# The conditioning of layer 0 in a two-layer hybrid backbone step: the shift as TensorE products, x loaded first, and half of the products issued between the input's products

## The chip, the core and the metric

The kernel runs on one core of a Trainium2 chip. The metric is the device time of one execution in microseconds (us), as the median of several runs. A core has five engines that each run their own instruction list in order and wait for one another through semaphores: TensorE (PE, matmuls; PEld are its weight loads), VectorE (DVE), ScalarE (ACT), GpSimd (POOL) and SyncE (SP), which here issues most of the DMA loads.

## What is computed

The reference is one step of a two-layer model on 512 latent and 128 context tokens, 640 in all, with 1024 channels. What the change touches is the start of layer 0: two vectors for each kind of token, a shift and a scale, are made from a conditioning vector, and the normalised input is modulated with them before the input projection.

```python
def branch_inputs(x, cond, w_ada, b_ada, norm_g, w_in):
    shift, scale, gate = jnp.split(jax.nn.silu(cond) @ w_ada + b_ada, 3, axis=-1)
    xm = rms_norm(x, norm_g) * (1.0 + scale) + shift
    parts = jnp.split(xm @ w_in, SPLIT_POINTS, axis=-1)
    return gate, parts
```

`cond` is `c` for the latent tokens and `c_ctx` for the context tokens, so each product with `w_ada` (1024 x 3072 for a layer) has two rows. All is fp32. After that come, in each layer, three token mixers (neighbourhood attention, latent attention, a Fourier mix), their gates and the output projections.

## The kernel before, in words

Activations stand with channels on the partitions: x is 8 tiles of 128 channels by 640 tokens, columns 0 to 511 latent and 512 to 639 context. An fp32 product is made of three matmuls of rounded parts: each operand is split in a high part (ScalarE copies it to `fp32r`) and a low part (VectorE or GpSimd subtracts the high part), and high x high, low x high and high x low are summed in PSUM. A weight unit of 1024 x 128 is loaded by `unit` (512 KB into `wr`), split by ScalarE into `wh` and by GpSimd into `wl`.

`start` does the conditioning of layer 0 and the first three weight units of the input projection (`ckv`, `ql0`, `ql1`; the last of them is split in halves into tiles named `k`). Its parts, with the line numbers of the kernel before:

- Loads (lines 285 to 290, and the string `ORD` from line 359 on): SyncE issues the eight x tiles with seven small loads between them, then follows `ORD`: A to D are four quarters of the scale part of `w_ada` (`wsc`, 8 tiles of 128 x 512 for each half of the channels), U the next weight unit, P the shift columns of channel tile 0 (`wsp`), S the transposed shift columns of one further channel tile (`wsh`).
- `cond` broadcast (lines 293 to 299): four matmuls with one row of ones (L295) put the conditioning vector on all partitions, and ScalarE's tanh (L297) and VectorE (L298) make silu of it (`sil`).
- `rms` (L177 to L192): ScalarE squares each x tile, VectorE adds them up, TensorE sums over the partitions with a matrix of ones, and the reciprocal root `y` is made from that (L164 to L167).
- `products` (L323): fp32 matmuls of `cc` (silu of the two conditioning rows, 128 x 2 for each k) with a weight tile, into two rows of PSUM; ScalarE copies the row (L325), TensorE transposes it in pieces of 128 (L327), and VectorE makes from them `am` = (1 + scale) x norm weight (L333), or `mod`, the shift of channel tile 0 (L331). There are 8 products of 512 columns for each half of the scale, and 8 of 128 columns for the shift of channel tile 0.
- `shift(n)` (L339): for the channel tiles 1 to 7 VectorE multiplies a transposed weight tile with `sil` and sums along the row, four times for a channel tile.
- `modulate` (L255, L259, L263, L265): VectorE forms h x am x y, ScalarE adds the shift, and the result is split in `xh` and `xl`; for a channel tile in `LOP` the low part is GpSimd's work (L144), else VectorE's. Then 18 matmuls of 320 columns (L390 to L392) add this channel tile to six accumulators in PSUM, two for each unit.

The code's order is only a wish: the build arranges each engine's list by its own schedule, so that matmuls of a channel tile can stand between products. `tc.issue_after(i)` keeps an instruction behind `i`. PSUM has eight banks: `s` takes two of them, `g` three, `pt` two and `o` one. The first matmul behind `start` is one of the units' gemms (L149, `g<-wh,xh` of 272 columns); from there on the two kernels have the same work.

Of the kernel before, what the change touches and what calls it, by code (L numbers as in the profile page):

```python
# [10 lines left out]
F32 = mybir.dt.float32  # L11
F32R = mybir.dt.float32r
AF = mybir.ActivationFunctionType
# [15 lines left out]
NS = 1  # L29
NF = (5, 4, 0, 0)  # L30
LOP = range(5)
# [7 lines left out]
ORD = "ASBSUPCUDSSSSUSS"  # L39
# [39 lines left out]
def step_kernel(ctx: ExitStack, tc: tile.TileContext, io):  # L79
# [197 lines left out]
    def start():  # L277
# [5 lines left out]
        rows = [sb_t("xl") for _ in range(4)]  # L283
        small = [(cc[:, 0], io["condT"])]
        small += [(rows[j][0:1, :512], io["cond"][j // 2:j // 2 + 1, (j % 2) * 512:(j % 2 + 1) * 512]) for j in range(4)]
        small += [(vecs, io["vecs"]), (bada, io["bada"])]
        for k in range(KD):
            sp.dma_start(out=h[k], in_=io["xt"][k])
            if k < len(small):
                sp.dma_start(out=small[k][0], in_=small[k][1])  # L290
        silu2(cc[:, 1], cc[:, 0])
        sil = []
        for j in range(4):
            g = psum("g" if j < 3 else "o")
            pe.matmul(g, ones[0:1], rows[j][0:1, :512], start=True, stop=True)  # L295
            t = sb_t("m", F32, 512)
            act.activation(out=t, in_=g, func=AF.Tanh, scale=0.5)  # L297
            dve.scalar_tensor_tensor(out=t, in0=t, scalar=1.0, in1=g, op0=ALU.add, op1=ALU.mult)  # L298
            sil.append(t)
        hg, gb = (sb.tile([128, KD], F32, name=n) for n in ("hg", "gb"))  # L300
        dve.tensor_scalar(hg, vecs[:, 0, 0:8], 0.5, None, ALU.mult)
        dve.scalar_tensor_tensor(out=gb, in0=bada[:, 0, 8:16], scalar=1.0, in1=vecs[:, 0, 0:8], op0=ALU.add, op1=ALU.mult)
        rms(h, 1.0 / D, y, ((0, T),), ("pt", "pt"))
        sc = psum("s")
        ws = []

        space = iter(["pt"] * 6 + ["q"] * 4 + ["lt"] * 5 + ["k"] + ["v"] * 8 + ["l"] * 2 + ["ob"] * 2 + ["gt"] + ["k"] * 4)
        wsc, wsh = [[], []], {}

        def load_scale(hf, ks):  # L310
            for k in ks:
                wsc[hf].append(sb_t(next(space))[:, :512])
                sp.dma_start(out=wsc[hf][k], in_=io["wsc"][hf, k])

        def load_shift(n):
            wsh[n] = [sb_t(next(space)) for _ in range(2)]
            for hf in range(2):
                sp.dma_start(out=wsh[n][hf][:, :512], in_=io["wsh"][n - NS, :, hf * 512:(hf + 1) * 512])

        def products(ws, n, col, n0):  # L320

            for k in range(KD):
                pe.matmul(sc[0:2, 0, :n * 128], cc[:, 1, k], ws[k], start=k == 0, stop=k == KD - 1)  # L323
            row = sb_t("fh")
            act.activation(out=row[0:2, :n * 128], in_=sc[0:2, 0, :n * 128], func=AF.Copy)  # L325
            for i in range(n):
                pe.transpose(sc[:, 1, col + 2 * i:col + 2 * i + 2], row[0:2, i * 128:(i + 1) * 128], ident[0:2, 0:2])  # L327
            for i in range(n):
                src, m = sc[:, 1, col + 2 * i:col + 2 * i + 2], n0 + i
                if col == 16:  # L330
                    dve.tensor_scalar(mod[:, 0, :, m], src, 0.5, bada[:, 0, m:m + 1], ALU.mult, ALU.add)  # L331
                else:
                    dve.tensor_scalar(am[:, 0, :, m], src, hg[:, m:m + 1], gb[:, m:m + 1], ALU.mult, ALU.add)  # L333

        def shift(n):
            for i in range(2):
                for hf in range(2):
                    col = mod[:, 0, i, n:n + 1]
                    dve.tensor_tensor_reduce(out=junk, in0=wsh[n][hf][:, :512], in1=sil[2 * i + hf], scale=0.5,  # L339
                                             scalar=bada[:, 0, n:n + 1] if hf == 0 else col,  # L340
                                             op0=ALU.mult, op1=ALU.add, accum_out=col)

        wsp = []
# [14 lines left out]

        later_shifts, names = iter(range(NS, KD)), iter(("ckv", "ql0", "ql1"))
        for o in ORD:  # L360
            if o in "ABCD":
                hf, q = divmod("ABCD".index(o), 2)
                load_scale(hf, range(4 * q, 4 * q + 4))
            elif o == "S":
                n = next(later_shifts, None)
                if n is not None:
                    load_shift(n)
            elif o == "U":
                ws.append(start_unit(next(names)))
            else:  # L370
                for k in range(KD if NS else 0):
                    wsp.append(sb_t("xh")[:, :NS * 128])
                    sp.dma_start(out=wsp[k], in_=io["wsp"][k])
        for n in later_shifts:
            load_shift(n)
        products(wsc[0], 4, 0, 0)
        if NS:
            products(wsp, NS, 16, 0)
        products(wsc[1], 4, 8, 4)
        xs = x_tiles()  # L380
        acc = [[psum("g"), psum("g")], [psum("g"), psum("o")], [psum("pt"), psum("pt")]]
        for n in range(KD):
            if n >= NS:
                shift(n)
            modulate(0, n, h[n], y, xs, ((0, T),), "pool" if n in LOP else "dve")
            for u in range(3):
                hi, lo = ws[u][0][n], ws[u][1][n]
                for i, (a, b) in enumerate(HALVES):
# [3 lines left out]
                    pe.matmul(o, hi, xs[1][n][:, a:b], start=False, stop=n == KD - 1)  # L392
# [712 lines left out]
```

## Time and profile before

| | before |
|---|---|
| median of 3 runs | 1474.37 us (1473.84 to 1475.03) |
| profiled execution | 1476.68 us |
| span of its trace | 1474.9 us, 1.8 us less |
| busy TensorE, VectorE, ScalarE, GpSimd | 96%, 65%, 48%, 35% |
| start (up to the first L149 matmul) | 0 to 69.3 us |

The span runs from the first to the last instruction of the profiled execution; the metric has some 1.8 us around it. A busy share is the time in which the engine had an instruction in work. TensorE's share is made of modelled ends of pipelined matmuls, so how long a row of matmuls takes is better read from the starts. Times in the trace are counted from the start of the span.

### The profile page before, as it was taken

What the parts mean: (1) busy time and instruction counts of PE and PEld (TensorE: products, weight loads), DVE (VectorE), ACT (ScalarE), POOL (GpSimd) and SP (SyncE); (2) the same over time, 40 slices, a digit from 0 to 9 for tenths busy, and PEclk for the clock granted to TensorE, in tenths of its full rate; (3) what the DMA queues carried; (4) which work ended last, traced back from release to release, by engine and by line L of the source; (5) the groups of instructions that cost most, each with busy time, mean ns of one, the idle gap of its engine ahead of it and who ended that gap; (6) DMA issues with size and microseconds to landing.
All of it is one profiled execution on the core that took longest, in us unless ns stands there. A gap on an engine that the chain in (4) does not pass through costs nothing.

```text
span 1474.9 us, 24841 instructions
## 1 busy us (share of the span) xinstructions
PE 1418.6 (96%) x9623; PEld 1368.5 (93%) x9623; DVE 955.0 (65%) x1903; ACT 705.7 (48%) x1440; POOL 512.0 (35%) x233
## 2 busy tenths in 40 slices
PE   7899999999999999989989999999999999999996
PEld 2799999999999899989989999999999999999996
DVE  7768567777648888784576554565643667753456
ACT  5353454554536565412355444554544565652243
POOL 3351222123232132247653423113222312224764
PEclk9999999999999999999999999999999999999998
DMA  9244224234334444764553322122232323355544
GB/s 322 108 145 134 96 95 137 73 114 137 127 123 132 143 144 133 235 220 160 191 183 92 110 78 100 59 79 91 75 132 101 95 98 123 122 171 208 163 160 144
DMA packets 84302, 197.33 MB, mean 134 GB/s; under 512 B 10068, under 2 KB 23764, under 8 KB 84184
## 3 DMA queue, kind: packets, MB, share of 16 engines
q1 hardware_dynamic: 76152, 178.71, 37.2%
q10 hardware_dynamic: 8032, 17.04, 3.0%
q8 instruction: 75, 1.23, 0.3%
q14 instruction: 43, 0.35, 0.1%
HBM read 165.67 MB, written 30.05 MB: 133 GB/s over the span
## 4 chain that ended last, share of the span: by engine, by line
PE 79%; DVE 10%; DMA 5%; issue 3%; ACT 1%; POOL 1%; SPq 0%; DVEq 0%; POOLq 0%; ACTq 0%
PE g L150 21%; PE g L151 21%; PE g L149 21%; PE pt L563 4%; DVE junk L242 2%; PE o L611 2%; PE o L612 2%; PE s L150 2%; PE s L151 2%; PE s L149 2%; DMA wr<-wt 1%; PE s L760 1%; PE s L761 1%; DMA ob<-br_d 1%; POOL wl L125 1%
## 5 line engine op out<-in xcount | busy, mean ns | idle before, releaser
L125 POOL TENSOR_TENSOR wl<-wr,wh 128x1024 fp32r<-128x1024 f32 (+2 forms) x173 | 427.2, 2474 | 896.9 <-ACT wh L124 842.8
L149 PE MATMUL g<-xh,wh 128*128 128x320 f32 (+2 forms) x1584 | 490.6, 310 | 4.3 <-DVE lt L416 2.7
L151 PE MATMUL g<-xh,wl 128*128 128x320 f32 (+2 forms) x1584 | 494.6, 312 | 0.0
L150 PE MATMUL g<-xl,wh 128*128 128x320 f32 (+2 forms) x1584 | 491.5, 311 | 0.0
L149 PEld LDWEIGHTS g<-xh,wh 128*128 128x128 f32 x1584 | 299.2, 189 | 7.4 <-issue 2.9
L151 PEld LDWEIGHTS g<-xh,wl 128*128 128x128 f32 x1584 | 299.3, 189 | 1.8 <-POOL wl L125 0.2
L150 PEld LDWEIGHTS g<-xl,wh 128*128 128x128 f32 x1584 | 298.2, 188 | 2.0
L124 ACT ACTIVATE wh<-wr 128x1024 fp32r<-128x1024 f32 (+2 forms) x173 | 182.3, 1055 | 177.3 <-PE g L150 91.0
L144 DVE TENSOR_TENSOR pt<-pt,pt 128x512 fp32r<-128x512 f32 (+2 forms) x176 | 101.2, 588 | 29.7 <-ACT pt L143 27.6
L678 DVE TENSOR_REDUCE st<-s 128x1 f32<-128x640 f32 x64 | 52.6, 822 | 96.4 <-PE s L151 96.1
L143 ACT ACTIVATE pt<-pt 128x512 fp32r<-128x512 f32 (+2 forms) x176 | 88.2, 517 | 52.2 <-PE pt L563 49.8
L549 DVE TENSOR_SCALAR p<-p,st 128x640 f32<-128x640 f32 (+3 forms) x160 | 101.3, 638 | 5.4 <-DVE st L548 0.5
L563 PE MATMUL pt<-ident,p 128*128 128x128 f32 x575 | 91.8, 273 | 1.2 <-DVE p L549 1.2
L150 PE MATMUL g<-wl,xh 128*128 128x272 f32 (+1 forms) x320 | 91.6, 286 | 0.7 <-POOL wl L125 0.7
L149 PE MATMUL g<-wh,xh 128*128 128x272 f32 (+1 forms) x320 | 91.3, 287 | 0.0
L151 PE MATMUL g<-wh,xl 128*128 128x272 f32 (+1 forms) x320 | 91.2, 286 | 0.0
L680 ACT ACTIVATE p<-s,st 128x640 f32<-128x640 f32 x64 | 50.9, 795 | 72.9 <-DVE st L678 72.6
L563 PEld LDWEIGHTS pt<-ident,p 128*128 128x128 f32 x575 | 71.9, 140 | 9.1 <-DVE p L549 1.4
L548 DVE RECIPROCAL st<-st 128x1 f32<-128x1 f32 x160 | 25.1, 160 | 61.5 <-ACT p L680 35.5
L242 DVE CUSTOM_DVE_ANT_0 junk<-a,sc,mod 128x512 bf16<-128x512 f32 x64 | 62.3, 974 | 3.8 <-DMA a<-wada 3.5
L149 PE MATMUL g<-k,wh 128*128 128x320 f32 (+2 forms) x176 | 57.0, 324 | 7.3 <-ACT xh L263 2.4
L782 ACT ACTIVATE p<-p,st 128x384 f32<-128x384 f32 (+1 forms) x64 | 42.8, 668 | 44.1 <-DVE st L780 43.9
(274 smaller groups left out, 2979.2 us busy)
## 6 DMA issues: line engine op xcount, KB each, us to landing
wr<-wt SPq DMA_DIRECT2D x158, 512.0 KB, 3.5
a<-wada SPq DMA_DIRECT2D x64, 256.0 KB, 2.8
gate_d<-lt ACTq DMA_DIRECT2D x48, 320.0 KB, 2.2
m<-bias SPq DMA_DIRECT2D x32, 320.0 KB, 3.2
br_d<-ob SPq DMA_DIRECT2D x24, 320.0 KB, 2.7
l<-br_d SPq DMA_DIRECT2D x16, 320.0 KB, 3.5
p<-gate_d SPq DMA_DIRECT2D x16, 320.0 KB, 6.9
lt<-gate_d SPq DMA_DIRECT2D x16, 320.0 KB, 4.4
```

What stands on the lines that cost most here:

```text
L124: act.activation(out=wh[:, :n], in_=r[:, :n], func=AF.Copy)
L125: pool.tensor_tensor(out=wl[:, :n], in0=r[:, :n], in1=wh[:, :n].bitcast(F32), op=ALU.subtract)
L143: act.activation(out=hi, in_=src, func=AF.Copy)
L144: (pool if e == "pool" else dve).tensor_tensor(out=lo, in0=src, in1=hi.bitcast(F32), op=ALU.subtract)
L149: pe.matmul(out, ah, bh, start=i == 0, stop=False)
L150: pe.matmul(out, ah, bl, start=False, stop=False)
L151: pe.matmul(out, al, bh, start=False, stop=i == n - 1)
L242: dve.tensor_tensor_reduce(out=junk, in0=w, in1=sc[:, i], scale=0.5, scalar=bada[:, l, n:n + 1] if kc == 0 else col, op0=ALU.mult, op1=ALU ...
L549: dve.tensor_scalar(P, P, r[:, 0:1], None, ALU.mult)
L563: i = pe.transpose(out, x, ident)
L678: dve.tensor_reduce(out=st[:, 0:1], in_=s[:, :, :H2], op=ALU.max, axis=AX.XY, negate=True)
L680: act.activation(out=x.rearrange("p (a b) -> p a b", a=2), in_=s[:, :, :H2], func=AF.Exp, bias=st[:, 0:1], accum_out=st[:, 1:2])
```

## The change

The scale and the shift now both come from `products`. `w_ada`'s scale and shift columns lie in `wad0` as four blocks of 512 columns: scale of channel tiles 0 to 3, shift of the same, scale of 4 to 7, shift of 4 to 7. `products(0)` and `products(1)` stand ahead of the modulation; `products(2)` is issued behind the last matmul of channel tile 1, and `products(3)` behind that of channel tile 3 (the diff's loop has n = 2 and 3; the build's order below shows where they come to stand). The broadcast of `cond`, `sil`, `shift(n)` and the `wsp` tiles are gone. SyncE loads `condT`, `vecs` and `bada`, then all of x, then the first unit and the blocks in the order that `ORD` gives (A and B are block 0, E and F block 1, C and D block 2, G and H block 3). `LOP` names the channel tiles 1, 3 and 5 instead of 0 to 4.

```diff
-NS = 1
-LOP = range(5)
+LOP = (1, 3, 5)
-ORD = "ASBSUPCUDSSSSUSS"
+ORD = "XUABUEFUCDGH"
...
-        for k in range(KD):
-            sp.dma_start(out=h[k], in_=io["xt"][k])
-            if k < len(small):
-                sp.dma_start(out=small[k][0], in_=small[k][1])
+        sp.dma_start(out=cc[:, 0], in_=io["condT"])
         silu2(cc[:, 1], cc[:, 0])
-        sil = []
-        for j in range(4):
-            g = psum("g" if j < 3 else "o")
-            pe.matmul(g, ones[0:1], rows[j][0:1, :512], start=True, stop=True)
...
+        def load_x():
+            sp.dma_start(out=vecs, in_=io["vecs"])
+            sp.dma_start(out=bada, in_=io["bada"])
             for k in range(KD):
-                pe.matmul(sc[0:2, 0, :n * 128], cc[:, 1, k], ws[k], start=k == 0, stop=k == KD - 1)
+                sp.dma_start(out=h[k], in_=io["xt"][k])
...
+        def products(j, behind=None):
+
+            g = psum("g") if j == 1 else sc[:, 0]
+            for k in range(KD):
+                if behind is None:
+                    pe.matmul(g[0:2], cc[:, 1, k], wad[j][k], start=k == 0, stop=k == KD - 1)
+                else:
+                    with tc.issue_after(behind):
+                        pe.matmul(g[0:2], cc[:, 1, k], wad[j][k], start=k == 0, stop=k == KD - 1)
             row = sb_t("fh")
...
-        def shift(n):
-            for i in range(2):
-                for hf in range(2):
-                    col = mod[:, 0, i, n:n + 1]
-                    dve.tensor_tensor_reduce(out=junk, in0=wsh[n][hf][:, :512], in1=sil[2 * i + hf], scale=0.5,
...
+        sc = psum("s")
+        rms(h, 1.0 / D, y, ((0, T),), ("pt", "pt"))
+        products(0)
+        products(1)
         xs = x_tiles()
         acc = [[psum("g"), psum("g")], [psum("g"), psum("o")], [psum("pt"), psum("pt")]]
         for n in range(KD):
-            if n >= NS:
-                shift(n)
+            if n in (2, 3):
+                products(n, last.ins)
             modulate(0, n, h[n], y, xs, ((0, T),), "pool" if n in LOP else "dve")
...
-                    pe.matmul(o, hi, xs[1][n][:, a:b], start=False, stop=n == KD - 1)
+                    last = pe.matmul(o, hi, xs[1][n][:, a:b], start=False, stop=n == KD - 1)
```

How the change moves instructions is read from the built lists. The first place is TensorE's list around the first matmuls of the input projection (`xh86` and `wh47` are channel tile 0 and the first unit; `xh54` to `xh56` are `wsp` tiles, `lt57` to `k60` scale tiles of the second half). Before:

```order
L327 MATMUL s33_171<-ident_63,fh84_296 128x2
L323 MATMUL s33_171<-lt57_218,cc_89 2x512
L323 MATMUL s33_171<-lt58_220,cc_89 2x512
L390 MATMUL g102_334<-xh86_318,wh47_198 128x320
L391 MATMUL g102_334<-xh86_318,wl48_199 128x320
L390 MATMUL g103_335<-xh86_318,wh47_198 128x320
L391 MATMUL g103_335<-xh86_318,wl48_199 128x320
L390 MATMUL g104_336<-xh86_318,wh62_228 128x320
L391 MATMUL g104_336<-xh86_318,wl63_229 128x320
L390 MATMUL o105_337<-xh86_318,wh62_228 128x320
L391 MATMUL o105_337<-xh86_318,wl63_229 128x320
L323 MATMUL s33_171<-lt59_222,cc_89 2x512
```

The matmuls of channel tile 0 stand there after the scale of the first half and the shift of tile 0, with the products of the second half (two ahead, the other six after its first eight matmuls). With the change (`m28` to `m31` are tiles of block 1, `fh65` and `fh67` the copied rows of blocks 0 and 1, `xh68` is channel tile 0):

```order
L308 MATMUL g66_248<-m28_143,cc_89 2x512
L308 MATMUL g66_248<-m29_145,cc_89 2x512
L315 MATMUL s53_193<-ident_63,fh65_238 128x2 x4
L308 MATMUL g66_248<-m30_147,cc_89 2x512
L308 MATMUL g66_248<-m31_149,cc_89 2x512
L315 MATMUL s53_193<-ident_63,fh67_257 128x2 x4
L361 MATMUL g84_283<-xh68_267,wh11_109 128x320
L362 MATMUL g84_283<-xh68_267,wl12_110 128x320
L361 MATMUL pt88_287<-xh68_267,k33_153 128x320
L362 MATMUL pt88_287<-xh68_267,k34_154 128x320
```

Sixteen products of 512 columns now stand ahead of channel tile 0, the transposes of block 0's row come two products before their end, and those of block 1 after it.

The second place is the same list at `products(3)` (`lt45` to `k52` are the tiles of block 3; `xh72` is channel tile 4):

```order
L363 MATMUL pt89_288<-xl79_278,k33_153 128x320
L311 MATMUL s53_193<-lt45_177,cc_89 2x512
L311 MATMUL s53_193<-lt46_179,cc_89 2x512
L311 MATMUL s53_193<-lt47_181,cc_89 2x512
L311 MATMUL s53_193<-l48_183,cc_89 2x512
L311 MATMUL s53_193<-l49_185,cc_89 2x512
L311 MATMUL s53_193<-ob50_187,cc_89 2x512
L311 MATMUL s53_193<-ob51_189,cc_89 2x512
L311 MATMUL s53_193<-k52_191,cc_89 2x512
L315 MATMUL s53_193<-ident_63,fh94_390 128x2 x4
L361 MATMUL g84_283<-xh72_271,wh11_109 128x320
```

The eight products and the four transposes of their row stand between the last matmul of channel tile 3 and the first of channel tile 4; before, nothing but matmuls of channel tiles stood there. `products(2)` stands in the same way between the channel tiles 1 and 2.

The third place is VectorE's list where the modulation begins (`p1` to `p4` are x tiles, `p9` is `y`). With the change:

```order
L321 TENSOR_SCALAR am_78<-s53_193,hg_93,gb_94 128x2 x4
L254 SCALAR_TENSOR_TENSOR t90_289<-p1_80,am_78,p9_88 128x512
L254 SCALAR_TENSOR_TENSOR t90_289<-p1_80,am_78,p9_88 128x128
L254 SCALAR_TENSOR_TENSOR t91_314<-p2_81,am_78,p9_88 128x512
L254 SCALAR_TENSOR_TENSOR t91_314<-p2_81,am_78,p9_88 128x128
L254 SCALAR_TENSOR_TENSOR t93_357<-p3_82,am_78,p9_88 128x512
L254 SCALAR_TENSOR_TENSOR t93_357<-p3_82,am_78,p9_88 128x128
L254 SCALAR_TENSOR_TENSOR t95_400<-p4_83,am_78,p9_88 128x512
L254 SCALAR_TENSOR_TENSOR t95_400<-p4_83,am_78,p9_88 128x128
L319 TENSOR_SCALAR mod_77<-s53_193,bada_72 128x2 x4
L264 SCALAR_TENSOR_TENSOR xl76_275<-t90_289,mod_77,xh68_267 128x512
L264 SCALAR_TENSOR_TENSOR xl76_275<-t90_289,mod_77,xh68_267 128x128
```

Before, the modulation of the second half came behind 23 of the 28 reduces of `shift`. This is the last piece ahead of it (`ob74` and `ob75` are transposed shift weights):

```order
L339 ISA junk_79,mod_77<-ob74_252,m15_113,bada_72 128x512
L339 ISA mod_77 128x1
L339 ISA junk_79,mod_77<-ob75_253,m17_118,mod_77 128x512
L339 ISA mod_77 128x1
L333 TENSOR_SCALAR am_78<-s33_171,hg_131,gb_132 128x2 x4
L339 ISA junk_79,mod_77<-ob74_252,m19_123,bada_72 128x512
L339 ISA mod_77 128x1
L255 SCALAR_TENSOR_TENSOR t112_456<-p5_84,am_78,p9_88 128x512
L255 SCALAR_TENSOR_TENSOR t112_456<-p5_84,am_78,p9_88 128x128
L255 SCALAR_TENSOR_TENSOR t113_485<-p6_85,am_78,p9_88 128x512
L255 SCALAR_TENSOR_TENSOR t113_485<-p6_85,am_78,p9_88 128x128
```

With the change no reduce stands between `am` and the modulation; `mod` of a half comes after the eight multiplications of its four channel tiles.

## Rows read from the trace of the kernel before

**Rows 1.** Busy time by stretch: length; PE, PEld, DVE, ACT, POOL; clock; DMA share; GB/s.

```profile
0.00:69.30 69.30, 53.40 (x213) 31.61 (x214) 54.76 (x107) 29.27 (x51) 23.03 (x17) 0.93 0.65 229
69.30:1474.90 1405.60, 1365.15 (x9412) 1336.87 (x9410) 900.28 (x1796) 676.46 (x1390) 489.01 (x216) 0.99 0.39 129
```

**Rows 2.** Waits of TensorE, 0 to 69.3 us: total, times, longest.

```profile
PE g L390 <- ACT xh L143: 6.4, 1, 6.4
...
PE s L323 <- DVE am L333: 2.8, 1, 2.8
```

**Rows 3.** Busy time of line L339 alone in the start (reduces, accumulator reads; DVE, clock, DMA).

```profile
0.00:69.30 69.30, 31.27 (x56) 0.93 0.65 229
```

**Rows 4.** Timeline of SyncE, ScalarE, VectorE: start, duration, engine, line, operation, tiles, idle before.

```profile
0.74 0.39 SPq L288 DMA_DIRECT2D p<-xt  x1
...
3.57 0.74 ACT L177 ACTIVATE t<-p 128x640 f32<-128x640 f32 x1 [1.56 <-DMA p<-xt]
...
13.04 0.82 DVE L185 TENSOR_TENSOR t<-t,t 128x640 f32<-128x640 f32 x1
```

**Rows 5.** Busy time in the stretch from 10 to 20 us, columns as in rows 1.

```profile
10.00:20.00 10.00, 9.86 (x17) 1.91 (x16) 8.72 (x21) 4.49 (x7) 0.00 (x0) 1.00 1.03 377
```

**Rows 6.** Timeline of TensorE in the start.

```profile
11.98 5.24 PE L323 MATMUL s<-pt,cc 128*2 128x512 f32 x6
17.15 1.34 PE L192 MATMUL pt<-t,onesr 128*128 128x320 f32 x4
...
19.28 3.60 PE L323 MATMUL s<-q,cc 128*2 128x512 f32 x8
23.64 0.38 PE L327 MATMUL s<-ident,fh 2*128 2x2 f32 x4 [0.77 <-ACT fh L325]
...
66.69 0.31 PE L390 MATMUL g<-xh,wh 128*128 128x320 f32 x1
...
69.32 0.29 PE L149 MATMUL g<-wh,xh 128*128 128x272 f32 x1
```

**Rows 7.** Timeline of ScalarE and VectorE around the modulation.

```profile
22.91 0.59 ACT L325 ACTIVATE fh<-s 2x512 f32<-2x512 f32 x1 [0.19 <-PE s L323]
25.97 0.83 DVE L333 TENSOR_SCALAR am<-s,hg,gb 128x2 f32<-128x2 f32 x4
26.72 3.78 DVE L255 SCALAR_TENSOR_TENSOR t<-p,am,p 128x512 f32<-128x512 f32 x8
...
35.42 0.72 ACT L259 ACTIVATE t<-t,mod 128x512 f32<-128x512 f32 x1 [1.18 <-DVE mod L339]
```

**Rows 8.** Busy time and granted clock in three stretches, columns as in rows 1.

```profile
56.40:69.30 12.90, 12.85 (x72) 12.85 (x73) 8.95 (x20) 4.22 (x10) 1.67 (x1) 0.81 0.01 2
...
27.00:28.00 1.00, 1.00 (x8) 0.67 (x7) 1.00 (x3) 0.41 (x1) 0.00 (x0) 0.65 1.04 375
...
55.00:61.00 6.00, 4.55 (x17) 4.55 (x18) 6.00 (x11) 3.29 (x7) 1.67 (x1) 0.50 0.08 31
```

**Rows 9.** Timeline of GpSimd and VectorE: a reduce beside GpSimd, and one without.

```profile
22.81 2.68 POOL L125 TENSOR_TENSOR wl<-wr,wh 128x1024 fp32r<-128x1024 f32 x1 [21.40 <-ACT wh L124]
23.33 2.70 DVE L339 CUSTOM_DVE_ANT_0 junk<-lt,m,mod 128x512 bf16<-128x512 f32 x1
...
51.73 0.75 DVE L339 CUSTOM_DVE_ANT_0 junk<-ob,m,mod 128x512 bf16<-128x512 f32 x1
```

**Rows 10.** Timeline of GpSimd, VectorE and TensorE near 130 us, and the stretch's clock.

```profile
127.75 4.88 POOL L125 TENSOR_TENSOR wl<-wr,wh 128x1024 fp32r<-128x1024 f32 x2 [20.77 <-ACT wh L124]
128.22 2.48 DVE L469 TENSOR_TENSOR t<-t 128x128 f32<-128x128 f32 x1
130.62 2.55 DVE L242 CUSTOM_DVE_ANT_0 junk<-a,sc,bada 128x512 bf16<-128x512 f32 x1
133.57 0.69 PE L151 MATMUL pt<-v,pt 128*128 128x128 f32 x2 [2.96 <-DVE pt L144]
...
130.00:140.00 10.00, 7.04 (x31) 6.74 (x31) 8.45 (x17) 1.51 (x4) 2.62 (x2) 0.66 0.51 157
```

More of the change, by code (lines that the diff above doesn't have):

```diff
@@ L282, in start @@
         cc = sb.tile([128, 2, KD, 2], F32, name="cc")
[L283 to L286, printed above, removed]
-        for k in range(KD):
-            sp.dma_start(out=h[k], in_=io["xt"][k])
-            if k < len(small):
-                sp.dma_start(out=small[k][0], in_=small[k][1])
@@ L310, in load_scale, with load_ada @@
-        def load_scale(hf, ks):
+        space = iter(["pt"] * 6 + ["q"] * 4 + ["m"] * 6 + ["v"] * 8 + ["lt"] * 3 + ["l"] * 2 + ["ob"] * 2 + ["k"])
+        wad = {}
+        def load_ada(i, ks):
             for k in ks:
[L312 to L316, printed above, removed]
-            for hf in range(2):
-                sp.dma_start(out=wsh[n][hf][:, :512], in_=io["wsh"][n - NS, :, hf * 512:(hf + 1) * 512])
@@ L320, in products @@
-        def products(ws, n, col, n0):
-            for k in range(KD):
-                pe.matmul(sc[0:2, 0, :n * 128], cc[:, 1, k], ws[k], start=k == 0, stop=k == KD - 1)
-            row = sb_t("fh")
[L325 to L330, printed above, removed]
+                t = sb_t(next(space))[:, :512]
@@ new lines, in products @@
+        def products(j, behind=None):
[6 more added lines that the diff above has]
+                        pe.matmul(g[0:2], cc[:, 1, k], wad[j][k], start=k == 0, stop=k == KD - 1)
+            row = sb_t("fh")
+            act.activation(out=row[0:2], in_=g[0:2], func=AF.Copy)
+            for i in range(4):
+                pe.transpose(sc[:, 1, 8 * j + 2 * i:8 * j + 2 * i + 2], row[0:2, i * 128:(i + 1) * 128], ident[0:2, 0:2])
+            for i in range(4):
+                src, m = sc[:, 1, 8 * j + 2 * i:8 * j + 2 * i + 2], 4 * (j // 2) + i
+                if j % 2:
@@ L357, in start_unit @@
             return out
-        later_shifts, names = iter(range(NS, KD)), iter(("ckv", "ql0", "ql1"))
+        names = iter(("ckv", "ql0", "ql1"))
         for o in ORD:
[L361 to L367, printed above, removed]
+            if o == "X":
+                load_x()
             elif o == "U":
@@ L370, in start @@
             else:
[L371 to L379, printed above, removed]
+                j, q = divmod("ABEFCDGH".index(o), 2)
+                load_ada(j, range(4 * q, 4 * q + 4))
+        sc = psum("s")
+        rms(h, 1.0 / D, y, ((0, T),), ("pt", "pt"))
+        products(0)
+        products(1)
         xs = x_tiles()
@@ L1045, in layout @@
     w0 = f["w_ada"][0]
[L1046 to L1048 removed]
+    o["wad0"] = np.ascontiguousarray(w0[:, :2 * D].reshape(KD, 128, 4, 512).transpose(2, 0, 1, 3)[[2, 0, 3, 1]])
     o["cond"] = np.stack([f["c"][0], f["c_ctx"]])
```

21 lines of the change are left out of this document (4 added, 17 removed).

## The prediction

> **What bounds the kernel now.** I read first the busy time of each engine by stretch, then TensorE's waits, then the timeline of the start, engine by engine. In the stretches, the first column is the length, and the busy times follow by engine. From 69.3 us on TensorE is busy 1365.15 of 1405.60 us (97%), VectorE 900.28 (64%); in the start, up to 69.3 us, TensorE is busy 53.40 of 69.30 [rows 1]. So the rest of the program is TensorE's, and the start is the one place where a change to conditioning can move the time: what counts is when the first L149 matmul runs, now at 69.32 us [rows 6].
>
> In the start TensorE waits twice for what the change touches: 2.8 us until VectorE has made `am` of the first half, and 6.4 us until ScalarE has the modulated tile 4 [rows 2]. The second wait stands behind VectorE: its 28 reduces of `shift` with their accumulator reads are 31.27 us of work in the start [rows 3], and the modulation of the second half is behind 23 of them. So before, VectorE and the loads that feed its reduces set the first 56 us, and TensorE's products fit into its waits.
>
> **What the change removes.** All 31.27 us of L339 go from VectorE, and the four broadcast matmuls with their tanh and silu steps. The wait of 6.4 us at tile 4 goes with them, since nothing but `am` stands ahead of the modulation. What comes in exchange is 16 more products of 512 columns on TensorE, for the 8 of 128 columns that go; TensorE is then what sets the start. So I add up its list from the first matmul on.
>
> **When TensorE starts.** The three small loads are issued ahead of x. The first load was issued at 0.74 and its tile was squared at 3.57, 2.83 later [rows 4]; with an issue taking 0.39 and the next one some 0.06 behind, x's first issue comes at about 2.1 and lands at 4.9. Seven more of 327,680 bytes at the 377 GB/s of the loaded stretch [rows 5] take 0.87 each: the last lands at 11.0. A square (0.74) and an addition (0.82) behind it [rows 4] give 12.6 for the sum over partitions. Bounds: 0.8 earlier at a rate above 400, 0.7 later if the small loads delay more.
>
> **The products ahead of tile 0.** A 512-column product is two entries: 8 entries in 3.60 us for the four `q` tiles, about 0.43 from start to start; the six entries at 11.98 took 5.24 until 17.15, 0.87 each, twice that [rows 6], although the granted clock of the stretch is written as 1.00 [rows 5]. TensorE had begun these products 5.2 us before it came to the full rate, and I let the new list run at half rate for the same 5.2 us, to 17.75 (bounds: no such time, which saves 1.6 us, and twice as long, which costs 2.6). Ahead of tile 0 stand four entries of the sum over partitions (1.34 us at full rate [rows 6], so 2.1 with the half rate and rounding, to 14.65) and 32 entries of products. 3.1 us at 0.87 do 3.6 of them, 28.4 at 0.43 take 12.2: 30.0. The transposes of the first row, 0.38 [rows 6], stand before the last four entries: first row at 28.6, last product at 30.4. The 16 weight tiles of 262,144 bytes, two units of 0.52 MB and x are 7.9 MB, 20.8 us at 377 GB/s, so they have landed by about 24 and TensorE doesn't wait for loads.
>
> **The first gap.** From 28.6 on: `am` until the next instruction 0.75, eight multiplications 3.78 [rows 7], the first `mod` about 0.2, ScalarE's 0.72 for the latent part of tile 0 [rows 7], 0.1 between engines: tile 0 starts at 34.2. TensorE stands from 30.4, less 0.4 of transposes of the second row: some 3.4 us, where before 2.8 stood.
>
> **The channel tiles and the rest of the products.** A tile's 18 matmuls take 2.63 us at the full clock (66.69 to 69.32 [rows 6]). Tiles 0 and 1: 5.3, and 0.5 (an estimate: ScalarE has seven instructions of up to 0.72 in that time) until the high part of tile 1 comes from ScalarE: 40.0. The clock: 72 matmuls in 12.90 us behind the 6.4 us wait [rows 8] are 2.4 more than 4 x 2.63; the granted clock in 55 to 61 us was 0.50, and 0.65 in the microsecond behind the 2.8 us wait [rows 8]. A gap between these in length costs between nothing and 2.4; I take 1.0, as it is nearer to the short one: 41.0. `products(2)`: 16 entries, 6.9: 47.9. Tiles 2 and 3 with four transposes inside, 5.3 + 0.4: 53.5. `products(3)`, 6.9: 60.4. Behind it a second gap, since the row must be copied, transposed and made `mod` before ScalarE can finish tile 4: 0.59 + 0.38 + 0.2 + 0.72 [rows 6, 7] and 0.3 between engines, 2.2: 62.6. (The second half's `am` and multiplications lie under `products(3)`: 4.5 us under 6.9. Without that cover they would add 4.5.) Tiles 4 to 7: 10.5, so **73.1** for the first L149 matmul, **3.8 us later** than 69.3.
>
> Edits that I cost at nothing: the two tiles fewer whose low part GpSimd makes (VectorE has 31 us free for them, GpSimd is waited for at neither place); the loads of blocks 2 and 3, which land by 36 us under the tiles and are wanted at 41 and 53.
>
> **The rest of the program.** It has the same instructions, and TensorE is busy 97% there, so I carry the delay to the end: span 1474.9 + 3.8 = 1478.7, profiled execution 1476.68 + 3.8 = 1480.5. That execution is 2.3 us above the median of the runs, 1474.37, so the time is 1474.37 + 3.8 = **1478.2**. A difference of 0.2% (2.95 us) is about what a measurement of this kernel can tell from none, so the forecast is just beyond it.
>
> **A lock between VectorE and GpSimd.** The reduce that started at 23.33 beside GpSimd's 22.81 to 25.49 took 2.70 us; the same reduce took 0.75 at 51.73 with GpSimd idle [rows 9]. So a VectorE instruction can lose 1.95 us to one of GpSimd. In the new list the third unit's low parts (loads until about 25, two GpSimd instructions behind ScalarE's) end close to 29.4, when the eight multiplications start, so I count nothing, and 1.95 as the bound. The Trainium skill's SBUF — State Buffer, section "Who interferes with whom", says that a VectorE instruction with two SBUF inputs and a GpSimd instruction that reads SBUF exclude each other, and that the one issued first blocks the other wholly. By that rule each multiplication, which reads x and `y`, would wait out a GpSimd instruction that is under way, and the sum is up to 1.95 higher, 1480.2; the rows of 23.33 and 51.73 agree with it.
>
> **The rivals.**
> - *The stall near 130 us goes.* There GpSimd's pair of L125 (4.88 us from 127.75) lies beside VectorE's L469 (2.48) and L242 (2.55), and TensorE waits 2.96 us for VectorE until 133.57; the granted clock of 130 to 140 us is 0.66, 3.4 us lost [rows 10]. The order around it isn't changed, but a load that lands at another moment against TensorE parts the two, and 2.96 + 3.4 = 6.4 come back: 1478.2 - 6.4 = 1471.8. It decides for faster if, besides, the start ends before 72.7. For it: the coincidence is of a few us. Against it: VectorE's and GpSimd's work there follow TensorE, which moves both. 0.17, of which 0.07 faster.
> - *The start ends no later.* No half rate at the beginning (-1.6), no lost clock after the gap (-1.0), tile 1 ready in time (-0.5): 70.0, and 1475.1. For it: nothing waits for VectorE any more; against it: the count of entries. 0.14, of which 0.02 faster.
> - *Cold and locked.* The lock (+1.95) and the long clock loss (2.4 in place of 1.0): 76.4, and 1481.5. 0.12.
>
> **How the numbers follow.** The forecast, start at 71.5 to 75 and the rest as before, has 0.57: 1476.6 to 1480.1, of which 0.40 lies beyond 1477.3 and 0.17 below. With the rivals: faster 0.07 + 0.02 = 0.09; same 0.17 + 0.10 + 0.12 = 0.39; slower 0.40 + 0.12 = 0.52. The range, 1473.0 to 1481.5, leaves out most of the first rival below and a little above.
>
> **What would show it.** Right: no L339 rows; product entries 0.43 apart; TensorE idle some 3.4 us before tile 0 and 2.2 before tile 4; the first L149 matmul near 73; the stall near 130 us there, some 4 us later. Wrong: that matmul at 70 or sooner, or a wait of more than 1 us gone from or new in the stretch behind the start.

## The result, and the profile after

| | before | after |
|---|---|---|
| median of 4 runs | 1474.70 us (1473.84 to 1476.48) | 1488.33 us (1485.36 to 1489.38) |
| ratio, with its 95% interval | | 1.0074 [1.0062, 1.0086] |
| profiled execution | 1476.68 us | 1487.6 us |
| span of its trace | 1474.9 us | 1485.8 us |
| first matmul behind the start | 69.32 us | 76.85 us |
| the rest, from there to the end | 1405.60 us | 1408.95 us |

The changed kernel is slower by 0.74%, some 10.9 us of 1474.7, where 3.8 were forecast: the direction held, the time lies outside the range. The two medians are 13.6 apart (0.92%), which is more than the ratio says; how the ratio weighs the runs is not on record. I go by the ratio, since the same kernel measured again (e8 below) gave 1.0070, and since the two spans are also 10.9 apart: 7.5 of it are the start, 3.4 the rest.

The stretches of after answer to [rows 1], [rows 5] and the stall in [rows 10]: length, busy time of PE, PEld, DVE, ACT and POOL with their instructions, then the granted clock, the DMA share and GB/s.

```profile
0.00:76.85 76.85, 56.48 (x229) 30.46 (x229) 27.17 (x58) 27.92 (x46) 15.66 (x15) 0.98 0.57 206
...
76.85:1485.80 1408.95, 1368.64 (x9412) 1341.06 (x9410) 902.40 (x1796) 675.59 (x1390) 489.39 (x216) 0.99 0.40 129
...
5.00:6.00 1.00, 0.00 (x0) 0.00 (x0) 0.00 (x0) 0.80 (x2) 0.00 (x0) 1.00 0.87 230
6.00:7.00 1.00, 0.00 (x0) 0.00 (x0) 0.36 (x1) 0.61 (x1) 0.00 (x0) 1.00 0.80 269
...
139.60:146.40 6.80, 5.52 (x21) 5.48 (x22) 5.68 (x15) 1.22 (x4) 0.33 (x1) 0.50 0.57 190
```

In the start VectorE's busy time is less than half of before's, as meant. In the rest the same 9412 matmuls were busy for 3.49 us more than before, and that is the whole growth of the rest (3.35).

TensorE's waits in after's start, then in its rest, then in before's rest (line, what it waited for: us in total, times, longest):

```profile
PE pt L191 <- DVE t L184: 15.1, 1, 15.1
PE g L361 <- ACT xh L262: 3.8, 2, 2.6
...
PE g L148 <- DVE v L143: 4.2, 3, 2.6
PE pt L150 <- DVE pt L143: 3.8, 2, 3.6
PE g L148 <- DVE lt L387: 3.0, 2, 2.7
```

```profile
PE g L149 <- DVE v L144: 4.5, 3, 2.6
PE g L149 <- DVE lt L416: 3.0, 2, 2.7
PE pt L151 <- DVE pt L144: 3.0, 1, 3.0
```

The 6.4 us at tile 4 of [rows 2] are gone; TensorE waits for x at the beginning instead, and twice for the modulation. The stall of [rows 10] is still there (3.6). No wait in the rest accounts for 3.4 us more: all those that are listed add up to 31.3 us in either kernel.

The timeline of after's start on TensorE (start, us, engine, line, operation, operands, shape, count, in brackets the idle time before it), against [rows 6]:

```profile
15.12 2.47 PE L191 MATMUL pt<-t,onesr 128*128 128x320 f32 x4 [15.12 <-DVE t L184]
...
30.92 0.41 PE L315 MATMUL s<-ident,fh 2*128 2x2 f32 x4
31.26 1.88 PE L308 MATMUL g<-m,cc 128*2 128x512 f32 x4
33.87 0.41 PE L315 MATMUL s<-ident,fh 2*128 2x2 f32 x4 [0.74 <-ACT fh L313]
36.92 0.41 PE L361 MATMUL g<-xh,wh 128*128 128x320 f32 x1 [2.65 <-ACT xh L262]
...
41.20 0.31 PE L361 MATMUL g<-xh,wh 128*128 128x320 f32 x1
...
43.93 7.03 PE L311 MATMUL s<-v,cc 128*2 128x512 f32 x16
50.89 0.42 PE L361 MATMUL g<-xh,wh 128*128 128x320 f32 x1
...
56.89 2.74 PE L311 MATMUL s<-lt,cc 128*2 128x512 f32 x6
...
66.19 0.41 PE L361 MATMUL g<-xh,wh 128*128 128x320 f32 x1 [1.14 <-ACT xh L262]
...
76.85 0.29 PE L148 MATMUL g<-wh,xh 128*128 128x272 f32 x1
```

The list runs as written down ahead, but from 15.12 on. ScalarE's squares of x, against [rows 4], say why:

```profile
4.94 0.74 ACT L176 ACTIVATE t<-p 128x640 f32<-128x640 f32 x1 [2.33 <-DMA p<-xt]
5.87 0.74 ACT L176 ACTIVATE t<-p 128x640 f32<-128x640 f32 x1 [0.20 <-DMA p<-xt]
8.73 1.56 ACT L176 ACTIVATE t<-p 128x640 f32<-128x640 f32 x2 [2.12 <-DMA p<-xt]
10.47 3.20 ACT L176 ACTIVATE t<-p 128x640 f32<-128x640 f32 x4 [0.18 <-DMA p<-xt]
```

The first tile comes at 4.94 as forecast (4.9). For the third ScalarE waits 2.12 us, until 8.73, where the forecast's count has 6.6: between 5 and 7 us the loads moved 230 and 269 GB/s, not 377. From the third on the squares stand back to back at 0.8.

### The profile page after: what moved, and what is told of

It reads as the page before. It is cut to its first block, busy times and chain, and to the rows that moved or that the text cites. A ratio compares the mean times of both kernels' runs of the same rounds, so it can differ in the third digit from the quotient of the medians.

```text
span 1485.8 us, 24807 instructions
## 1 busy us (share of the span) xinstructions
PE 1425.1 (96%) x9638; PEld 1371.5 (92%) x9638; DVE 929.6 (63%) x1854; ACT 703.5 (47%) x1435; POOL 505.1 (34%) x231
## 4 chain that ended last, share of the span: by engine, by line
PE 79%; DVE 9%; DMA 5%; issue 3%; ACT 2%; POOL 1%; SPq 0%; DVEq 0%; ACTq 0%; POOLq 0%
PE g L148 20%; PE g L149 20%; PE g L150 20%; PE pt L534 4%; DVE junk L241 2%; PE o L583 2%; PE o L582 2%; PE s L150 2%; PE s L149 2%; PE s L148 1%; DMA a<-wada 1%; PE s L311 1%; PE s L732 1%; PE s L731 1%; DMA wr<-wt 1%
## 5 line engine op out<-in xcount | busy, mean ns | idle before, releaser
L519 DVE RECIPROCAL st<-st 128x1 f32<-128x1 f32 x160 | 25.1, 160 | 61.6 <-ACT p L651 35.4
L380 ACT ACTIVATE lt<-g 128x320 f32<-128x320 f32 x96 | 41.0, 428 | 47.5 <-PE g L150 47.2
```

## The experiments

Seventeen kernels besides the changed one, and the changed one again (e8). Each ratio is to before on the same chip; e1 to e4 were timed on one chip, e5 to e8 and e15 on a second, e9, e10, e12 and e13 on a third, e14 on a fourth. "Start" is the time of the first matmul behind the start. "At half" adds up the stretches of the rest, up to the end of the span, in which the granted clock is 0.50 (1.2 of 2.4 GHz). "Spacing" is the mean from one start to the next over all pairs of neighbouring TensorE starts of the rest that are 136 to 150 ns apart (some 5,700 pairs, nearly all matmuls of 320 columns); "short" the share under 143 ns. "Places" are the addresses of the buffers `xh`, `xl`, `wh`, `wl` in a partition, modulo 128 bytes, as the build assigned them.

| kernel | ratio to before | start | rest | at half | spacing, short | places |
|---|---|---|---|---|---|---|
| before | 1 | 69.32 | 1405.60 | 24.2 | 145.72, 13.8% | 0 64 0 0 |
| after | 1.0074 | 76.85 | 1408.95 | 21.8 | 146.56, 1.6% | 0 0 0 0 |
| after again (e8) | 1.0070 [1.0056, 1.0083] | 76.14 | 1408.56 | 20.1 | 146.57, 1.5% | 0 0 0 0 |
| e1 | 1.0045 [1.0029, 1.0060] | 74.70 | 1409.30 | 21.4 | 146.58, 1.4% | 0 0 0 0 |
| e2 | 1.0048 [1.0035, 1.0062] | 76.33 | 1407.37 | 14.7 | 146.58, 1.4% | 0 0 0 0 |
| e3 | 1.0044 [1.0030, 1.0058] | 74.16 | 1408.04 | 20.3 | 146.57, 1.5% | 0 0 0 0 |
| e4 | 1.0035 [1.0024, 1.0046] | 79.27 | 1400.43 | 14.2 | 145.76, 13.2% | 0 64 0 0 |
| e5 | 1.0075 [1.0059, 1.0091] | 76.40 | 1407.30 | 20.1 | 146.57, 1.5% | 0 0 0 0 |
| e6 | 1.0045 [1.0027, 1.0063] | 76.82 | 1404.88 | 20.5 | 145.74, 13.5% | 0 64 0 0 |
| e7 | 1.0039 [1.0025, 1.0053] | 70.62 | 1411.28 | 26.8 | 146.57, 1.5% | 0 0 0 0 |
| e9 | 1.0037 [1.0022, 1.0051] | 76.02 | 1401.88 | 17.6 | 145.73, 13.9% | 64 0 64 64 |
| e10 | 1.0027 [1.0018, 1.0036] | 70.49 | 1413.01 | 25.0 | 146.58, 1.5% | 0 0 0 0 |
| e12 | 1.0033 [1.0021, 1.0045] | 72.71 | 1408.79 | 23.9 | 145.72, 13.9% | 0 64 0 0 |
| e13 | 1.0007 [0.9997, 1.0017] | 73.03 | 1402.37 | 20.6 | 145.73, 13.8% | 0 64 0 0 |
| e14 | 1.0028 [1.0016, 1.0040] | 70.30 | 1407.00 | 24.1 | 145.75, 13.5% | 0 64 0 0 |
| e15 | 0.9988 [0.9977, 0.9998] | 67.49 | 1407.41 | 27.0 | 145.75, 13.4% | 0 64 0 0 |

### The start, three parts alone

**e1** turns block 0's row behind the third product of block 1, not behind the sixth, so that `am` is ready sooner.

```diff
-                if behind is None:
+                if behind is None or (j == 1 and k < 3):
...
-        products(0)
-        products(1)
+        products(1, products(0).ins)
```

> The change, with the transposes of block 0's row put behind the third product of block 1 instead of the sixth, so that VectorE makes am and the multiplications under the remaining products. Theory 1 (the rest of the program follows the end of the start one to one): the gap ahead of channel tile 0 shrinks from 3.4 to about 2 us, the start ends about 1.5 us earlier, near 75.3, and the time is about 1486.8. Theory 2 (behind the start the loss depends on which instructions happen to meet): the start ends as said, but the time lies anywhere from 1483 to 1490.

**e2** issues `products(3)` ahead of channel tile 3 and its transposes a third into that tile.

```diff
-                    pe.matmul(o, hi, xs[0][n][:, a:b], start=n == 0, stop=False)
+                    with tc.issue_after((turned if u else done)[0]) if n == 3 else contextlib.nullcontext():
+                        pe.matmul(o, hi, xs[0][n][:, a:b], start=n == 0, stop=False)
```

> The change, with products(3) put ahead of channel tile 3 and its transposes a third into that tile, so that the copy, the transposes and mod lie under matmuls. Theory 1: the gap of 2.3 us ahead of channel tile 4 goes, the start ends near 74.6 and the time is about 1486.1. Theory 2: the start ends as said, the time lies anywhere from 1482 to 1490.

**e3** issues the three small loads behind x.

```diff
-        sp.dma_start(out=cc[:, 0], in_=io["condT"])
...
             for k in range(KD):
                 sp.dma_start(out=h[k], in_=io["xt"][k])
+            sp.dma_start(out=cc[:, 0], in_=io["condT"])
```

> The change, with the three small loads issued behind x instead of ahead of it. If their 384 short packets are what made x late, TensorE starts 1.2 to 1.5 us earlier than 15.1, the start ends near 75.5 and by theory 1 the time is about 1487.0. If the late x comes from the rate of the queue or from the long issue near 4.4 us, TensorE starts at 14.5 or later and the time stays near 1488.

e1 shortened the first gap (waits for the modulation 2.5 in all, the longest 1.4, where after has 3.8) and ended the start 2.2 us sooner, of which 0.4 lie ahead of what it changes (TensorE began at 14.72). e2 removed the second gap, but its start ended only 0.5 sooner: there is a TensorE wait of 1.0 for `am`, and 6.8 us at the half clock where after has 3.4. These begin at 35.4, ahead of what e2 changes, so they are not shown to come from it. In e3 the squares of x were

```profile
3.66 0.74 ACT L176 ACTIVATE t<-p 128x640 f32<-128x640 f32 x1 [1.65 <-DMA p<-xt]
...
6.99 1.56 ACT L176 ACTIVATE t<-p 128x640 f32<-128x640 f32 x2 [1.53 <-DMA p<-xt]
```

so x came sooner, by 1.3 us at the first tile and 1.7 from the third on, and ScalarE again waited for the third (1.53), with nothing small ahead of it. TensorE began at 13.38, 1.7 sooner and more than either expectation had, and the start ended 2.7 sooner. All three were measured 0.22 to 0.3% (3.2 to 4.4 us) better than the changed kernel, which for e2 above all is more than its start moved; why is not settled (after itself was not timed on their chip). But none came near to before, and none changed the spacing in the rest.

### Is a delay of the start carried to the end?

**e4** is before with 36 more products of 128 columns ahead of channel tile 7 (their sums are not read).

```diff
+            if n == KD - 1:
+                for i in range(36):
+                    with tc.issue_after(last):
+                        pad = pe.matmul(sc[0:2, 0, :128], cc[:, 1, i % 8], ident, start=True, stop=True).ins
```

> The kernel before with 36 small extra products (128 columns, result not read) ahead of channel tile 7, which delay the end of the start by some 7.5 us, as the change does; the instructions behind the start come to stand in the order that they have in the changed kernel. Theory 1: 1474.7 + 7.5 = 1482.2, with the start ending near 77. Theory 2 (the delay or the new order behind the start costs more by itself): 1485 to 1489, as the changed kernel, though nothing of the change is in it.

The start ended at 79.27, later than in after, and the time grew by only 0.35%, half of what after lost and less than either theory had. With a later start TensorE was busy for less time in the same 9412 matmuls:

```profile
79.27:1479.70 1400.43, 1361.43 (x9412) 1332.75 (x9410) 901.83 (x1796) 676.46 (x1390) 487.96 (x216) 0.99 0.39 130
```

So a later start does not by itself make the rest longer: after's rest had something of its own, and the spacing was where it showed: its neighbouring matmuls were 0.84 ns further apart.

### Where the buffers lie

A tag's buffers get their address when the program first asks for the tag, and the change asks in another order: `xl` moved from 28224 to 196480, `xh` from 146304 to 176000, `wh` from 120192 to 41344, `wl` from 133248 to 54400, and the PSUM banks changed too. Of the kernels that follow, e5, e6 and e9 issue on every engine what after issues, in its order, and e7 and e10 what before does; only places differ. **e5** gives after the PSUM banks of before, **e6** its SBUF places; **e7** gives before the SBUF places of after. **e8** is after again, on the same chip.

```diff
+        for tag in ("xl", "m"):
+            for _ in range(BUFS[tag]):
+                sb_t(tag)
+        hg, gb = (sb.tile([128, KD], F32, name=n) for n in ("hg", "gb"))
+        for tag in ("t", "pt", "q", "lt", "wr", "wh", "wl", "xh", "k", "v", "l", "ob", "gt", "fh"):
+            for _ in range(BUFS[tag]):
+                sb_t(tag)
```

(e6; the others ask in other orders, e5 for `psum` tags.)

> The changed kernel, instruction for instruction, with its PSUM tiles in the banks of the kernel before (g in 0 to 2 and not in 4 to 6). Behind the start the matmuls of the changed kernel follow each other 146.6 ns apart, those of the kernel before 145.7, of which one in seven is 140. Theory 3a (the banks set that spacing): mean 145.7, the rest of the program about 8 us shorter, some 1479 against the changed kernel's 1487 on this chip. Theory 3b (the SBUF addresses set it) and theory 3c (it goes with the start's instructions): spacing and time as the changed kernel's.

> The changed kernel, instruction for instruction, with its SBUF tiles at the addresses of the kernel before (a tag's place follows from the order in which tags are first used, which the change turns round). Theory 3b (SBUF addresses set the spacing): mean 145.7 ns, the rest of the program near 1400.5 us as in the padded kernel, and about 8 us less than the changed kernel. Theory 3a and 3c: 146.6 ns and the changed kernel's time.

> The kernel before, instruction for instruction, with its SBUF tiles at the addresses of the changed kernel. Theory 3b: the spacing rises from 145.7 to 146.6 ns and the time by about 8 us, with nothing else of the change in it. Theory 3a and 3c: as the kernel before, ratio within 0.15% of 1.

> The changed kernel once more, beside the three others on one chip. Its first runs gave 1.0074 (1.0062 to 1.0086); I expect the same ratio within 0.2%, spacing 146.6 ns, start ending near 76.8 us.

The banks do nothing. The SBUF places take the spacing from 146.6 to 145.7 in after and the other way in before; the rows are e6's, and then e7's:

```profile
76.82:1481.70 1404.88, 1363.50 (x9412) 1335.36 (x9410) 905.45 (x1796) 676.83 (x1390) 489.30 (x216) 0.99 0.39 129
```

```profile
70.62:1481.90 1411.28, 1371.75 (x9412) 1343.87 (x9410) 902.66 (x1796) 678.40 (x1390) 489.89 (x216) 0.99 0.38 129
```

PE's busy time is 5.1 us less in e6 than in after, and 6.6 more in e7 than in before. In time both moved by less than the 8 us that I had expected: 0.25% (3.7 us) against e8, and 0.39% (5.8). What of the places counts? `hg` and `gb` take 64 bytes together, and everything asked for behind them is moved by as much. **e9** puts them between `xh` and `xl` in after, **e10** ahead of `xl` in before, where only `xl` and `m` move, by 64 bytes.

```diff
         cc = sb.tile([128, 2, KD, 2], F32, name="cc")
+        hg, gb = (sb.tile([128, KD], F32, name=n) for n in ("hg", "gb"))
         rows = [sb_t("xl") for _ in range(4)]
```

> The changed kernel, instruction for instruction, with the two small tiles hg and gb (64 bytes together) placed between xh and xl instead of ahead of wr: all big tiles but xl stand 64 bytes lower, xl where it stood. In the kernel before xl stands at 64 modulo 128 bytes and xh, wh and wl at 0; in the changed kernel all four stand at 0. Theory 3d (xl against the others modulo 128 sets the spacing): 145.7 ns, and a ratio near 1.0045 instead of 1.0070. Theory 3e (the region of SBUF in which a tile lies sets it): 146.6 ns and 1.0070.

> The kernel before, instruction for instruction, with hg and gb placed ahead of xl: xl and m stand 64 bytes higher, nothing else moves. Theory 3d: xl then stands at 0 modulo 128 as the others, the spacing rises to 146.6 ns and the time by 4 to 6 us (ratio 1.003 to 1.004). Theory 3e: 145.7 ns and no change.

64 bytes decide it. Before, at a place that both kernels reach at the same time, and e10 there:

```profile
218.03 0.30 PE L149 MATMUL g<-xh,wh 128*128 128x320 f32 x1
218.17 0.31 PE L150 MATMUL g<-xl,wh 128*128 128x320 f32 x1
218.31 0.31 PE L151 MATMUL g<-xh,wl 128*128 128x320 f32 x1
218.46 0.30 PE L149 MATMUL g<-xh,wh 128*128 128x320 f32 x1
```

```profile
218.03 0.31 PE L149 MATMUL g<-xh,wh 128*128 128x320 f32 x1
218.18 0.31 PE L150 MATMUL g<-xl,wh 128*128 128x320 f32 x1
218.32 0.31 PE L151 MATMUL g<-xh,wl 128*128 128x320 f32 x1
218.47 0.31 PE L149 MATMUL g<-xh,wh 128*128 128x320 f32 x1
```

The step behind a matmul with `xh,wh`, to one with `xl`, is 0.14 in before and 0.15 in e10; over a triple 0.43 against 0.44. Over the whole rest that step is where the difference lies: its mean is 143.3 ns in before, with 48% of the steps under 143, and 146.5 in e10, with 2%; the other two steps of a triple have 145.9 and 147.3 in before, 146.6 both in e10. Nothing else in the program changes, and by the timed runs it costs e10 4.0 us (0.27%) and e7 5.8 (0.39%), though their profiled starts also ended 1.2 and 1.3 later.

Which pair has to lie apart? Four kernels that ran once each, all before with places moved: `xh` by 64 (**p1**), `wl` by 64 (**p2**), `wh` by 64 (**p3**), `xl` by 32 (**q1**), for p1 to p3 with one or two pads of 64 bytes among the requests.

```diff
+        sb.tile([128, 16], F32, name="pad1")
```

> The kernel before, instruction for instruction, with xh (and what lies behind it) 64 bytes higher: xh and xl at 64 modulo 128, wh and wl at 0. If the spacing hangs on xh against xl (two moving operands that follow each other under the same weights), the matmuls of xh by wh lose their short gaps: mean 146.6 ns. If it hangs on xl against the weights wh: 145.7 ns as in the kernel before.

> The kernel before with wl 64 bytes higher against wh and xh: wl and xl at 64 modulo 128, wh and xh at 0. If xh against xl decides: 145.7 ns, short gaps behind the matmuls of xh by wh alone. If weights against moving operands count too, the matmuls of xh by wl get short gaps as well and the mean falls below 145.2 ns.

> The kernel before with wh 64 bytes higher: wh and xl at 64 modulo 128, wl and xh at 0. If xh against xl decides: 145.7 ns. If xl against wh decides: 146.6 ns.

> The kernel before, instruction for instruction, with hg alone ahead of xl: xl and m stand 32 bytes higher, at 96 modulo 128. If only the 64-byte half in which xl lies against the others counts, 145.7 ns stay; if any move from the 64-byte place loses the short gaps, 146.2 ns or more.

| | xh xl wh wl | spacing | rest |
|---|---|---|---|
| p1 | 64 64 0 0 | 146.52 | 1408.09 |
| p2 | 0 64 0 64 | 146.42 | 1411.43 |
| p3 | 0 64 64 0 | 146.26 | 1408.32 |
| q1 | 0 96 0 0 | 146.27 | 1406.44 |

By the spacing each costs most of the gain, so neither of the pairs proposed (`xl` against `xh`, `xl` against the weights) does it alone: of the places tried, only those with `xl` 64 bytes apart from all three kept the short steps, and 96 (q1), in the same half of 128 bytes, lost them. In p1 another step is the short one, from `xl,wh` to `xh,wl` (144.0), and the first has 148.1. Why is left open.

### Mending the start

**e13** keeps all four blocks of products, with e1's transposes, before's places, and the small loads on ScalarE's queue.

```diff
-        sp.dma_start(out=cc[:, 0], in_=io["condT"])
+        act.dma_start(out=cc[:, 0], in_=io["condT"])
...
-        products(0)
-        products(1)
+        products(1, products(0).ins)
```

> The changed kernel with early transposes, x ahead (small loads on ScalarE's queue) and the addresses of the kernel before; all products stay. Start ends near 72.5 (76.5 less 2.0 for the transposes and 2.0 for x), 3.2 later than before, spacing 145.7: ratio 1.002. If it were below 1.000 the products would cost less than counted.

1.0007: no longer to be told from before. TensorE began at 13.08, the start ended at 73.03, and the rest was short:

```profile
73.03:1475.40 1402.37, 1363.01 (x9412) 1335.47 (x9410) 903.92 (x1796) 676.45 (x1390) 488.38 (x216) 0.99 0.38 129
```

**e12** also gives the shift of tiles 4 to 7 back to VectorE (16 reduces, the broadcast of `cond` that they need, no `products(3)`), with seven small loads on ScalarE's queue; **e14** is e12 with before's order of loads, and the reduces of tiles 6 and 7 behind the second `am`; **e15** moves those behind tile 4's low part, and the transposes of `products(2)` into tile 2. The first cut below is e12 against after, the other two e15 against e14 and after.

```diff
-            if n in (2, 3):
+            if n == 2:
                 products(n, last.ins)
+            if n >= 4:
+                shift(n)
...
-                    with tc.issue_after((shifted if n < 6 else scaled)[0]):
+                    with tc.issue_after(shifted[0] if n < 6 else lowered[4]):
...
+                    with tc.issue_after(turned_at[2]) if n == 2 and u else contextlib.nullcontext():
```

> A version made of what the runs showed: x ahead and the small loads on ScalarE's queue; products for the scale of both halves and the shift of the first half; the shift of channel tiles 4 to 7 as 16 VectorE reduces behind the first half's mod; the first transposes early; addresses as in the kernel before. From the parts: the start of the run with early transposes ended at 74.7; less 2 for x, 7.0 for products(3) and 2.3 for the gap behind it gives 63.4, 6 us before the kernel before's 69.3, with its spacing: ratio about 0.996. Rival: the 16 reduces (12 us and more beside GpSimd) end late and channel tile 4 waits, start ends at 66 to 68, ratio 0.998 to 1.000.

> The version with the second half's shift on VectorE, with the loads of x and the small ones in the order of the kernel before (on ScalarE's queue the small rows held x up by 6 us), and the reduces of channel tiles 6 and 7 behind the second half's am. TensorE's sum over partitions at about 14.0 instead of 19.2, no wait of 1.8 at channel tile 4: the start ends near 66 to 67.5, 2 to 3 us before the kernel before's, with its spacing: ratio 0.997 to 0.999. Rival: the reduces and the lock with GpSimd hold channel tile 4 up all the same: 69 and 1.000.

> The version with the second half's shift on VectorE again, with the transposes of products(2) inside channel tile 2 and the reduces of channel tiles 6 and 7 behind the low part of tile 4. The 1.1 and 2.9 us that TensorE waited at channel tile 4 go: the start ends at 65 to 67, some 3 to 4 us before the kernel before's, with its spacing of 145.7 ns. If the rest behind the start is 1401 to 1405 us, the span is 1467 to 1472 and the ratio 0.996 to 0.999; if the rest comes out at 1407 as in the run before, 1473 and 0.999 to 1.000.

e12 missed by its loads. ScalarE's silu of `cond` stands ahead of the squares of x, and its load, issued at 3.51, let it begin only at

```profile
9.23 0.21 ACT L223 ACTIVATE cc<-cc 128x16 f32<-128x16 f32 x1 [2.80 <-DMA cc<-condT]
9.35 3.90 ACT L180 ACTIVATE t<-p 128x640 f32<-128x640 f32 x6
```

so the sum over partitions came at 19.22. With before's loads it came at 14.54 in e14, which missed too (1.0028): it now waited for a low part queued behind the moved reduces:

```profile
PE g L406 <- DVE xl L268: 2.9, 1, 2.9
```

e15 has neither the late sum nor that wait, ends its start at 67.49, and is the one version faster than before, by just more than the noise: 0.9988 [0.9977, 0.9998], about 1.8 us.

```profile
67.49:1474.90 1407.41, 1365.79 (x9412) 1338.65 (x9410) 906.45 (x1796) 678.82 (x1393) 489.47 (x216) 0.99 0.38 129
```

## Why the prediction was right and where it was wrong

**What bounds the kernel, and what the change removes**: right. The reduces are gone, the wait of 6.4 with them, and TensorE's own list sets the start.

**When TensorE starts**: wrong by 2.5 of the 3.7 us by which the start was missed (76.85 against 73.1). "Seven more ... at the 377 GB/s of the loaded stretch [rows 5] take 0.87 each" took the rate of a full queue for the first microseconds. The third tile was 2.1 us behind that count, and ScalarE (0.8 a square) and VectorE could not make it up: 15.12, not 12.6. The bound given, 0.7, was too narrow. The small loads are not the main part of it: in e3, with none ahead, the same count has the third tile at 5.3, and it was squared at 6.99, still 1.7 late.

**The products, the gaps, the tiles**: right part by part, once by luck. From TensorE's first matmul to the last product ahead of tile 0 the sum had 17.8 and the trace has 17.9 (31.26 and four entries of 0.43, less 15.12); from the first row's transposes to tile 0 both have 5.6; tiles 0 and 1 took 7.0 for 6.8 (where two errors cancel: tile 0 took 4.28 from 36.92 to 41.20, 3.4 of it at the half clock, 1.65 over its 2.63, where 1.0 was counted, and the wait of 0.5 for tile 1 did not come), `products(2)` 6.96 for 6.9, tiles 2 and 3 6.0 for 5.6, `products(3)` with the second gap 9.3 for 9.1, tiles 4 to 7 10.7 for 10.5. Small excesses make up the other 1.2.

**The rest of the program**: "It has the same instructions, and TensorE is busy 97% there, so I carry the delay to the end" is the step that failed. The instructions are the same, but here the matmuls' pace went with where their operands lay (146.56 against 145.72 ns), and the change moved them. The price: 0.84 ns on some 5,700 spacings are 4.8 us. By timed runs it is 0.25 to 0.38%, 3.7 to 5.6 us, when the changed kernel (1.0070 to 1.0075) loses it again (e6 1.0045, e9 1.0037), and 4.0 to 5.8 when before gets it (e10, e7). What is left, 1.0037 to 1.0045, is 5.5 to 6.6 us for a start 6.7 to 7.5 later: within the intervals (some 2 us either way) the start and the places together are what was measured.

The step has a second weakness, which moving the places back does not mend. In kernels with before's places a later start was not carried through one to one either: e4's time grew by 5.2 us (3.5 to 6.8) for a start 9.95 later, e14's by 4.1 (2.4 to 5.9) for a start 1.0 later, over ten and twelve runs (the starts are those of one profiled execution each). So the length of the rest also depends, by some microseconds, on what stands in front of it; how is not shown.

In the profiled pair the rest grew by 3.35 only, and before's had more time at the half clock (24.2 against 21.8 us). Take half of that time off each rest in the large table, as if it had run at full rate: the eight kernels with `xl` apart (before, e4, e6, e9, e12 to e15) then have 1392.0 to 1396.9, mean 1394.1, the eight others 1397.2 to 1400.6, mean 1398.6. The groups don't overlap, though by little. The short rests of e4, e9 and e13 are in good part such time saved (14.2, 17.6 and 20.6 at half); how much of it is order and how much chance of one execution stays open.

**The lock**: the bound was not needed. The eight multiplications took 3.78 from 32.20, behind GpSimd's work, as counted. It struck elsewhere, on VectorE and then GpSimd of after:

```profile
32.20 3.78 DVE L254 SCALAR_TENSOR_TENSOR t<-p,am,p 128x512 f32<-128x512 f32 x8
...
40.24 3.14 DVE L264 SCALAR_TENSOR_TENSOR xl<-t,mod,xh 128x512 fp32r<-128x512 f32 x2 [2.32 <-ACT xh L262]
```

```profile
28.27 2.50 POOL L143 TENSOR_TENSOR k<-wr,k 128x512 fp32r<-128x512 f32 x2 [3.93 <-ACT k L142]
39.67 3.56 POOL L143 TENSOR_TENSOR xl<-t,xh 128x640 fp32r<-128x640 f32 x2 [8.91 <-ACT xh L142]
```

The low part that began at 40.24 took 3.14, where the one at 36.90 took 1.02, and ended 0.15 behind GpSimd's pair (43.23). The Trainium skill's SBUF — State Buffer, section "Who interferes with whom", has a VectorE instruction with two SBUF inputs and a GpSimd instruction that reads SBUF exclude each other; this trace agrees. It lay under the matmuls of tiles 0 and 1 and cost nothing, since it belongs to tile 2, which TensorE began only at 50.89, behind `products(2)`.

**The rivals**: none came about. The stall near 130 us moved with the rest and stayed, with 6.8 us at the half clock as before (139.6 to 146.4), though its price was not as fixed as the rival's sum had it: 3.4 us at the half clock follow it in e6 and e9, and none in p3 and q1, where the wait is 1.8 and 2.0; the start ended later, not sooner; "cold and locked" named neither cause of the loss.

## What to carry to other kernels

Moving work off a busy engine that is waited for helps only until the next list is the longer one; half of the moved work, with before's places and order of loads (e15), came out 0.12% faster, and all of it, with before's places and the small loads on ScalarE's queue (e13), came out even. A price for the first loads should come from the first microseconds of a trace, not from a loaded stretch. And before a delay is carried through code that is "the same", compare the buffers' addresses: a kernel that changes the order of first requests has moved its operands, and a timed comparison of the change then measures that too, unless a version with the old places is run beside it. Even with the old places, a delay of a few microseconds at the start need not come out whole at the end (e4, e14).

## What the runs showed that I had not expected

- The spacing of 320-column matmuls went with the addresses of the operands modulo 128 bytes: 145.7 ns where `xl` lay 64 apart from `xh`, `wh` and `wl`, 146.3 to 146.6 at every other placement tried, 4 to 6 us of 1475. PSUM banks made no difference (146.57 and 146.57).
- x's loads slowed to 230 to 269 GB/s some three microseconds after their first issue, with small loads ahead (5 to 7 us) or not (230 and 241 in e3, 4 to 6 us); in e3 they moved 320 and more before and after that.
- A small load issued on another queue while x was under way was used 5.7 us after its issue (e12), 1.6 when it was issued first (after: issue 0.74, use 2.39).
